# A half tile's rows join the joint expert query, are gathered after it, and 72 instead of 80 hidden blocks are stored

## The chip, the cores and the metric

The kernel runs on one core of one Trainium2 chip. Its metric is the time of one execution in device microseconds. The time before the change is 3701.82 us, the median of three runs (3690.5 to 3702.95).

## The reference

One layer of a hybrid decoder is computed for 1024 prompt tokens and for 64 sample tokens (8 sequences of 8 tokens), with the same weights. What matters here is its expert mixer:

```python
q = (xb @ wq).reshape(PEER_BLOCK, PEER_HEADS, 2, PEER_DKEY // 2)
s = jnp.einsum('phcd,hcnd->phcn', q, keys).astype(jnp.float32)
sv, si = lax.top_k(s, PEER_TOPK)
cand = sv[:, :, 0, :, None] + sv[:, :, 1, None, :]
cv, ci = lax.top_k(cand.reshape(PEER_BLOCK, PEER_HEADS, PEER_TOPK * PEER_TOPK), PEER_TOPK)
...
gsm = jax.nn.softmax(cv, axis=-1)
hval = jnp.einsum('pd,phkd->phk', xb, u_tab[e])
act = (jax.nn.gelu(hval.astype(jnp.float32), approximate=False) * gsm).astype(xb.dtype)
return jnp.einsum('phk,phkd->pd', act, v_tab[e])
```

For each token and each of 8 heads, 16 of 16384 experts are chosen by two lists of 128 keys. Each chosen expert has a row of 1024 numbers in `peer_u` and one in `peer_v`. Ahead of the mixer stand a norm, one input projection, a retention and a recurrence (RWKV) over the tokens, an output projection and a second norm. Behind it stand a gated per-layer embedding and the last norm.

## The kernel before, in words

The 1088 tokens are nine tiles: tiles 0 to 7 of 128 prompt tokens, and tile 8, a half tile of the 64 sample tokens. The kernel treats the tiles in three sets.

- `E0 = [0, 1, 8]`, the early tiles: each has a query of its own (`early_query`, line 1203) and then its experts' rows are **gathered**, all while the recurrence of later tiles runs (generator `early`, line 1251).
- `G1 = [2, 3]`: they take part in the joint query and are gathered late.
- `G2 = [4, 5, 6, 7]`: they take part in the joint query, and their mixer is **dense**: all 16384 experts, in 128 blocks of 128, are multiplied with these 512 tokens, and a table of gates that is zero for experts not chosen weighs them.

A *gather* (`gather`, line 1143) goes over the columns of the index table `eid`. For each, POOL issues one indirect DMA (line 1154) that fetches 128 rows of 1024 numbers, one for each partition. A whole tile has 128 columns in `peer_u` and 128 in `peer_v`. Tile 8 has 64 of each, since its 64 tokens lie twice on the partitions. DVE multiplies a `peer_u` row with the token and sums it (line 1168), and adds a weighted `peer_v` row to the sum `gacc` (line 1182). `gacc` is one buffer in PSUM, so gathers of tiles follow each other. In all there are 1152 gathers.

The stages, in order of time:

1. Projections of all tiles, then the **recurrence** (`group_b`), one tile after another in the order 1, 8, 2, 3, 4, 5, 6, 7. A tile's step finishes its state at line 932. Gathers of tiles 0 and 1 run beside it. Once tile 8's normed rows are there (`self.rowed`), `early` steps tile 8's query between tile 1's gathers (lines 1267 to 1275): 16 products of the half tile with a 1024 x 128 piece of the query weights (line 1232), a product with the keys (line 1235), five DVE instructions a piece that pick the 16 best of 128 (`pick`, lines 1046 to 1050), and the selection (`topk`).
2. The **joint query** (`c_query`, line 1017): for each of 16 pieces of the query weights, which are split into a high and a low part (POOL's `wql`, line 308), one product with the rows of `G1` (256 columns) and one with those of `G2` (512), a product with the keys each, and `pick` for each of the six tiles.
3. The **gates stage** (loop at line 1584). For each tile of `G2`: its selection, and its gates as one-hot products (`oh` on DVE, line 1297; scaling on ACT, line 1299; `pwt` on PE, line 1302; a copy on ACT, line 1303). `NPRE` hidden blocks are spread over it (`hidden`, line 1311): a block's 512 KB of `peer_u` are loaded on SP's queue, split by ACT and POOL (`ul`, line 308), multiplied on PE in 24 matmuls (`ph`) and stored in DRAM (`gd`, line 1591). At `TK1` = step 1 and step 4 the selection and the gather of tiles 2 and 3 are entered.
4. The **fused dense stage** (`dense_fused`): the other 128 - `NPRE` hidden blocks are made and used at once, four to a group, with 24 matmuls `py` each (lines 1353 to 1356).
5. The **stored dense stage** (`dense_stored`): the `NPRE` stored blocks are read back and used, five to a group. A group has 8 slices of `peer_v`; each is split (`vl` on POOL) and its product is added to `yT` on DVE (line 1360).
6. The **last stage** (`ple`): the per-layer embedding and the last norm, tile by tile in the order `E0 + G2 + G1`. The last tile, 3, adds its gathered sum straight from `gacc` (line 1446).

The program is written as Python generators, and a scheduler puts every engine's instructions in a fixed order from them. So what stands next to what on an engine is fixed ahead of the run, and an engine that comes to a gather's sum waits for it.

Of the kernel before, what the change touches and what calls it, by code (L numbers as in the profile page):

```python
# [9 lines left out]
F32 = mybir.dt.float32  # L10
# [3 lines left out]
U32 = mybir.dt.uint32  # L14
AF = mybir.ActivationFunctionType
# [154 lines left out]
PE_ = 0  # L170
PG = 0
PWS = 4
NPRE = 80
NF = 4
TK1 = {2: 1, 3: 4}
GEB = 2
GHB = 2
WQ = 32
# [1 line left out]
WB = 2  # L180
AB = 8
CRING = 4
E0 = [0, 1, 8]
G1 = [2, 3]
DW = 4
LW = 3
CN = 4
# [9 lines left out]
G2 = [4, 5, 6, 7]  # L197
# [3 lines left out]
QB = 4  # L201
SB = 3
EB = 150
SIZE = {t: (64 if t == 8 else 128) for t in range(9)}


def spans(tiles):

    e = [sum(SIZE[t] for t in tiles[:i]) for i in range(len(tiles) + 1)]
    return dict(zip(tiles, e)), e[-1]  # L210
# [8 lines left out]
class K:  # L219
# [797 lines left out]
    def c_query(self, wp, da, parts):  # L1017

        nc, I = self.nc, self.I
        for hc in range(16):  # L1020
            kT = wp.tile([128, 128], F32, name="keysT")
            nc.sync.dma_start(kT, I['keysT'][:, hc])
            raw = da.tile([128, 8, 128], F32, name="wqr", tag="uraw", bufs=UB)
            nc.sync.dma_start(raw, I['wq'][hc])
            wh = da.tile([128, 8, 128], F32R, name="wqh", tag="uh", bufs=DW)
            wl = da.tile([128, 8, 128], F32R, name="wql", tag="ul", bufs=LW)
            self.split(wh, wl, raw, "g")
            for tiles, x in parts:
                off, n = spans(tiles)
                s = wp.tile([128, len(tiles), 128], F32, name=f"ss{tiles[0]}", bufs=SB)  # L1030
                p = self.ps("pq", "b")
                self.mm3(p[:, :n], lambda k: wh[:, k, :], lambda k: wl[:, k, :], lambda k: x[0][:, k], lambda k: x[1][:, k], 8)
                qT = wp.tile([128, n], F32, name=f"qT{tiles[0]}", bufs=1)
                nc.scalar.activation(qT, p[:, :n], AF.Copy)
                p = self.ps("psc", "a")
                for i, t in enumerate(tiles):
                    nc.tensor.matmul(p[:SIZE[t], i * 128:i * 128 + 128], qT[:, off[t]:off[t] + SIZE[t]], kT, start=True, stop=True)
                nc.scalar.activation(s, p[:, :len(tiles) * 128].rearrange("p (t k) -> p t k", k=128), AF.Copy)
                for i, t in enumerate(tiles):
                    self.pick(self.found[t], hc, s[:, i], 128)  # L1040
            yield

    def pick(self, found, hc, s, n):
# [8 lines left out]
    def topk(self, tp, t, s=None, tags={}, ce=None):  # L1052
        nc = self.nc
        n = SIZE[t]
        if s is None:
            sv, si = self.found[t]
        else:
            sv = tp.tile([128, 16, 16], F32, name="sv")
            si = tp.tile([128, 16, 16], U32, name="si")
# [36 lines left out]
        cf = tp.tile([128, 128], F32, name="cf", tag="cf" if ce else "sf")  # L1096
# [9 lines left out]
        if t in G2:  # L1106
            gsm = self.gsm[t] = tp.tile([128, 128], F32, name="gsm", bufs=2)
            self.e12[t] = tp.tile([128, 2, 128], F32, name="e12", bufs=2)
        elif t == 8:
            gsm = tp.tile([128, 128], F32, name="gsm8", tag="cf")  # L1110
        else:
            gsm = self.gsm[t]
        ex = tp.tile([128, 8, 16], F32, name="ex")
# [137 lines left out]
    def early(self, wp):  # L1251

        rows = ("V", "V", "Wq", "Wq", "Wq", "Wq", "W", "xy")
        self.wide = True
        yield from self.early_query(wp, E0[0], "Wq", QB, (("W",), ("xy",)))
        g = self.gather(wp, E0[0], rows, acc=self.acc)
        while E0[1] not in self.rowed:
            next(g, None)
            yield
        self.wide = False  # L1260
        for i, _ in enumerate(self.early_query(wp, E0[1], "Wq", QB, ("Wq", "xT"))):
            if i % 3 == 0:
                next(g, None)
            yield
        yield from g
        g = self.gather(wp, E0[1], rows, acc=self.acc)
        q = None
        for i, _ in enumerate(g):
            yield
            if E0[2] in self.rowed and q is None:  # L1270
                q = self.early_query(wp, E0[2], "Wq", QB, ("Wq", "xT"))
            if q and i % 1 == 0:
                next(q, None)
        for _ in q:
            yield
        self.wide = False
        yield from self.gather(wp, E0[2], rows + ("xT",), acc=self.acc)

    def gates(self, wp, t, extra):
        nc = self.nc  # L1280
# [201 lines left out]
    def build(self):  # L1482
        PS = bass.MemoryType.PSUM
        run = lambda g: [None for _ in g]
        sb = lambda name, es, **kw: self.pool(name, es=es, reuse_waits="tile", **kw)
        with self.es:
            self.setup()
            em, ee, eg, et, ew, ex, ep, e0, e1, e2 = (ExitStack() for _ in range(10))
            acc = self.acc = self.pool("psumg", space=PS, es=eg, reuse_waits="tile")
# [12 lines left out]
            m = mix[0]  # L1502
# [16 lines left out]
            for _ in a:  # L1519
                for _ in range(IE):  # L1520
# [7 lines left out]
            parts = [G1, G2]  # L1528
            self.layout(cq, [(f"ss{g[0]}", [128, len(g), 128], F32, SB) for g in parts] +
                        [(f"qT{g[0]}", [128, spans(g)[1]], F32, 1) for g in parts])  # L1530
            c1 = sb("cx1", ew, side="right")
            x1 = self.rows_of(c1, G1)
            cx = sb("cx2", ex)
# [1 line left out]
            da = sb("dna", eg, bufs=2)  # L1535
            self.layout(da, [("uh", [128, 8, 128], F32R, DW), ("ul", [128, 8, 128], F32R, LW), ("uraw", [128, 8, 128], F32, UB), ("spare", [128, 8, 128], F32, 1)])
            tp = sb("tk", et)
            self.found = {t: (tp.tile([128, 16, 16], F32, name=f"sv{t}"), tp.tile([128, 16, 16], U32, name=f"si{t}")) for t in G1 + G2}
            self.e12 = {}
            n3 = spans(G2[:-1])[1]  # L1540
            query = self.c_query(cq, da, [(G1, x1), (G2, x)])
# [16 lines left out]
            run(ahead)  # L1558
            run(last)
            run(query)  # L1560
            run(early)
            ew.close()
            ee.close()
# [10 lines left out]
            with ExitStack() as e:  # L1574
                self.psums("psumw", e, i=1, w=2)
                self.psh = self.pool("psumh", bufs=3, space=PS, es=e, reuse_waits="tile")
                gw = sb("gw", e, side="right")
                self.stage = (gw, kp)
                self.turn = 0
                self.layout(gw, [("oh", [128, 2, 4, 128], F32, 2), ("it", [128, 128], F32, 2)])  # L1580
                gh = sb("gh", e, bufs=2, side="right")
                gate = iter(())
                nh = 0
                for i, t in enumerate(G2 + [None]):
                    tk = self.topk(tp, t) if t is not None else iter(())
                    while True:
                        a, b = next(tk, "end"), next(gate, "end")
                        if a == "end" and b == "end":
                            break
                    while nh < NPRE * (i + 1) // (len(G2) + 1):  # L1590
                        self.nc.scalar.dma_start(self.gd[nh], self.hidden(da, gh, x, nh))
                        nh += 1
                    gate = self.gates(gw, t, da) if t is not None else gate
                    for t in G1:
                        if i == TK1[t]:
                            run(self.topk(tp, t))
                            run(self.behind(self.gather(gp, t, acc=acc), PG))
            et.close()
            self.first = True
# [31 lines left out]
```

## Time and profile before

| | |
|---|---|
| median of three runs | 3701.82 us |
| profiled execution, its own time | 3682.12 us |
| its span | 3680.3 us |
| PE / DVE / POOL / ACT busy | 89% / 78% / 64% / 33% |
| moved by DMA | 1074.69 MB, 292 GB/s over the span |
| gathers (line 1154) | 1152, from 441.9 to 3635.6 us |
| stored blocks `gd` | 80 of 256 KB |

Times are in microseconds from the start of the span, unless marked as nanoseconds. PE is the matmul engine, and PEld is its weight load, which overlaps it. Matmuls are pipelined, so that a matmul's own duration is longer than the distance to the next. A row of a group gives the line, engine, operation, output and inputs, shapes, the count, then the busy time and the mean duration in nanoseconds, then the engine's idle time ahead of these instructions and what ended it. The granted clock is that of PE, 1.00 being full speed. The DMA share is the mean busy share of the core's 16 DMA engines.

### The profile page before, as it was taken

To read this page: it belongs to the slowest core of one execution; us is meant where nothing else is said; L and a number is where in the kernel's file an instruction comes from. 1 tells how busy PE (TensorE), PEld (TensorE's weight loads), DVE (VectorE), ACT (ScalarE), POOL (GpSimd) and SP (SyncE) were. 2 spreads that over 40 slices of the span, in tenths; PEclk is the share of its full clock that TensorE was granted. 3 is DMA by queue.
4 is the path that set the end of the run, shared out by engine and by line. 5 is a ranking of instruction groups with operands and counts; after the bars stand their busy time and mean duration, and the time that the engine had idled before them with its cause. 6 is when DMAs were issued, how large, how long until landed. Compare 5 with 4: busy or idle time off the path is not lost. (4 is left out here: it accounts for less than half of the span.)

```text
span 3680.3 us, 52362 instructions
## 1 busy us (share of the span) xinstructions
PE 3268.2 (89%) x17749; PEld 2715.5 (74%) x17749; DVE 2857.6 (78%) x5655; ACT 1218.4 (33%) x2259; POOL 2345.1 (64%) x2068
## 2 busy tenths in 40 slices
PE   8798996887968888876989999999999998899988
PEld 7697995654846667655877887887888877667766
DVE  4544689897797886688997999776777787778887
ACT  4233221111211211112333887773333333333322
POOL 5352677554355654436468777768888878887752
PEclk9798996666968885877999999999999999999999
DMA  7257599889858887878678988999999999999974
GB/s 263 86 192 244 200 350 316 277 300 309 280 187 308 311 298 238 300 252 295 206 261 310 324 311 287 345 350 355 342 346 339 332 364 353 369 361 365 340 246 167
DMA packets 423558, 1074.69 MB, mean 292 GB/s; under 512 B 46267, under 2 KB 143289, under 8 KB 418618
## 3 DMA queue, kind: packets, MB, share of 16 engines
q0 software_dynamic: 165888, 604.05, 45.9%
q1 hardware_dynamic: 202670, 377.02, 30.9%
q10 hardware_dynamic: 54732, 90.26, 6.6%
q8 instruction: 141, 2.31, 0.3%
q14 instruction: 127, 1.04, 0.1%
HBM read 980.93 MB, written 90.18 MB: 291 GB/s over the span
## 5 line engine op out<-in xcount | busy, mean ns | idle before, releaser
L1154 POOL DMA_INDIRECT grow<-in_pv,eid x576 | 569.5, 989 | 534.4 <-DVE gacc L1182 299.0
L1154 POOL DMA_INDIRECT grow<-in_pu,eid x576 | 564.2, 979 | 343.1 <-DVE grow L1168 203.2
L1168 DVE SCALAR_TENSOR_TENSOR grow<-grow,gacc 128x1024 f32<-128x1024 f32 x576 | 690.2, 1212 | 116.7 <-DMA grow<-in_pu,eid 114.9
L1182 DVE SCALAR_TENSOR_TENSOR gacc<-grow,ac,gacc 128x1024 f32<-128x1024 f32 x571 | 731.1, 1280 | 33.2 <-DMA grow<-in_pv,eid 28.2
L1353 PE MATMUL py<-ah,vh 128*128 128x512 f32 x1024 | 406.8, 398 | 32.2 <-ACT vh L304 32.2
L333 PE MATMUL ph<-cx,uh 128*128 128x512 f32 x1024 | 406.8, 397 | 7.2 <-DVE al L306 4.6
L334 PE MATMUL ph<-cx,uh 128*128 128x512 f32 x1024 | 405.0, 396 | 0.0
L1354 PE MATMUL py<-al,vh 128*128 128x512 f32 x1024 | 404.7, 395 | 0.0
L308 POOL TENSOR_TENSOR vl<-vraw,vh 128x640 fp32r<-128x640 f32 (+1 forms) x224 | 325.9, 1461 | 39.9 <-ACT vh L304 30.2
L308 POOL TENSOR_TENSOR ul<-uraw,uh 128x1024 fp32r<-128x1024 f32 x128 | 308.1, 2407 | 49.1 <-ACT uh L304 21.0
L1356 PE MATMUL py<-ah,vl 128*128 128x512 f32 x1024 | 272.3, 397 | 13.9 <-POOL vl L308 13.8
L336 PE MATMUL ph<-cx,ul 128*128 128x512 f32 x1024 | 263.4, 395 | 0.0
L1353 PEld LDWEIGHTS py<-ah,vh 128*128 128x128 f32 x1024 | 196.0, 191 | 82.0 <-ACT vh L304 40.3
L304 ACT ACTIVATE vh<-vraw 128x640 fp32r<-128x640 f32 (+1 forms) x224 | 154.8, 692 | 274.3 <-DMA vraw<-in_pvd 95.9
L1356 PEld LDWEIGHTS py<-ah,vl 128*128 128x128 f32 x1024 | 192.3, 189 | 63.3 <-POOL vl L308 21.7
L333 PEld LDWEIGHTS ph<-cx,uh 128*128 128x128 f32 x1024 | 194.8, 190 | 47.0 <-DVE al L306 5.0
L1360 DVE TENSOR_TENSOR yT<-yT,py 128x512 f32<-128x512 f32 x216 | 147.5, 684 | 102.1 <-PE py L1356 101.0
L1354 PEld LDWEIGHTS py<-al,vh 128*128 128x128 f32 x1024 | 195.8, 191 | 41.1
L334 PEld LDWEIGHTS ph<-cx,uh 128*128 128x128 f32 x1024 | 194.5, 190 | 38.5
L336 PEld LDWEIGHTS ph<-cx,ul 128*128 128x128 f32 x1024 | 191.3, 189 | 38.2
L304 ACT ACTIVATE uh<-uraw 128x1024 fp32r<-128x1024 f32 x128 | 135.0, 1056 | 162.0 <-DMA uraw<-in_puT 109.3
L1297 DVE TENSOR_TENSOR oh<-csta,pit 128x1024 f32<-128x1024 f32 x128 | 153.6, 1210 | 27.5 <-ACT oh L1299 17.9
(402 smaller groups left out, 7247.9 us busy)
## 6 DMA issues: line engine op xcount, KB each, us to landing
uraw<-in_puT SPq DMA_DIRECT2D x128, 512.0 KB, 4.2
vraw<-in_pvd SPq DMA_DIRECT2D x128, 320.0 KB, 7.2
cw<-in_w_out SPq DMA_DIRECT2D x128, 256.0 KB, 5.9
wd<-wst ACTq DMA_DIRECT2D x28, 1024.0 KB, 12.3
wt<-wd SPq DMA_DIRECT2D x64, 448.0 KB, 6.8
wraw<-in_w_ret SPq DMA_DIRECT2D x48, 512.0 KB, 4.2
ewq<-in_wq SPq DMA_DIRECT2D x48, 512.0 KB, 5.0
vraw<-in_pvd SPq DMA_DIRECT2D x96, 256.0 KB, 5.4
```

Source lines behind the costliest of these rows:

```text
L304: nc.scalar.activation(hi, src, AF.Copy)
L308: nc.gpsimd.tensor_tensor(lo, src, hi.bitcast(F32), op=OP.subtract)
L333: mm(out, lh(k), rh(k), start=first and k == 0, stop=False)
L334: mm(out, *((ll(k), rh(k)) if right else (lh(k), rl(k))), start=False, stop=False)
L336: mm(out, *((lh(k), rl(k)) if right else (ll(k), rh(k))), start=False, stop=last and k == nk - 1)
L1154: nc.gpsimd.indirect_dma_start(out=g, out_offset=None, in_=src, in_offset=bass.IndirectOffsetOnAxis(ap=self.eid[t][:, j:j + 1], axis=0))
L1168: nc.vector.scalar_tensor_tensor(g[:, c], g[:, c], 1.0, x[:, c], op0=OP.mult, op1=OP.mult, accum_out=hv[:, i, j:j + 1])
L1182: nc.vector.scalar_tensor_tensor(y[:, c], g[:, c], ac[:, j:j + 1], y[:, c], op0=OP.mult, op1=OP.add)
L1297: nc.vector.tensor_tensor(oh, io, p[:, 0:2, s + b:s + b + 4, None].to_broadcast([128, 2, 4, 128]), op=OP.is_equal)
L1353: nc.tensor.matmul(p, vh[:, b, :], ah, start=b == 0, stop=False)
L1354: nc.tensor.matmul(p, vh[:, b, :], al, start=False, stop=False)
L1356: nc.tensor.matmul(p, vl[:, b, :], ah, start=False, stop=b == nb - 1)
```

## The change

Tile 8 leaves the early set and becomes the first of the late set `G1`. Its rows are the first 64 of 320 columns in the joint query's first part. Its scores are copied by an ACT instruction of their own, over 64 partitions, and `pick` works on 64 partitions for it. Its selection is entered right behind the joint query, ahead of what is left of `early`, which is the rest of tile 1's gather. Its gather is entered in the gates stage at step 0, behind the first 14 hidden blocks. Tiles 2 and 3 keep their steps 1 and 4. `NPRE` goes from 80 to 72. So the fused stage has 56 blocks in 14 groups, and the stored stage has 72 in 15 groups, of which the last has two blocks. In the last stage tile 8 now stands behind tiles 4 to 7.

```diff
-NPRE = 80
+NPRE = 72
-TK1 = {2: 1, 3: 4}
+TK1 = {8: 0, 2: 1, 3: 4}
...
-E0 = [0, 1, 8]
-G1 = [2, 3]
+E0 = [0, 1]
+G1 = [8, 2, 3]
...
-                nc.scalar.activation(s, p[:, :len(tiles) * 128].rearrange("p (t k) -> p t k", k=128), AF.Copy)
+                m = len([t for t in tiles if t == 8])
+                for t in tiles[:m]:
+                    nc.scalar.activation(s[:64, 0], p[:64, :128], AF.Copy)
+                nc.scalar.activation(s[:, m:], p[:, m * 128:len(tiles) * 128].rearrange("p (t k) -> p t k", k=128), AF.Copy)
                 for i, t in enumerate(tiles):
-                    self.pick(self.found[t], hc, s[:, i], 128)
+                    self.pick(self.found[t], hc, s[:, i], SIZE[t])
...
-            gsm = tp.tile([128, 128], F32, name="gsm8", tag="cf")
+            gsm = tp.tile([128, 128], F32, name="gsm8", tag="gsm", bufs=2)
...
         g = self.gather(wp, E0[1], rows, acc=self.acc)
-        q = None
-        for i, _ in enumerate(g):
-            yield
-            if E0[2] in self.rowed and q is None:
-                q = self.early_query(wp, E0[2], "Wq", QB, ("Wq", "xT"))
-            if q and i % 1 == 0:
-                next(q, None)
-        for _ in q:
-            yield
         self.wide = False
-        yield from self.gather(wp, E0[2], rows + ("xT",), acc=self.acc)
+        yield from g
...
             run(query)
+            run(self.topk(tp, 8))
             run(early)
...
                         if i == TK1[t]:
-                            run(self.topk(tp, t))
+                            if t != 8:
+                                run(self.topk(tp, t))
                             run(self.behind(self.gather(gp, t, acc=acc), PG))
```

Tile 8's tables of scores found (`sv`, `si`) get a pool of their own, `cf8`, and the rows `cx` of `G1` are 320 wide. Line numbers after the change are 3 higher than before from `pick` on, and 6 lower from `gates` on.

More of the change, by code (lines that the diff above doesn't have):

```diff
@@ L1530, in build @@
                         [(f"qT{g[0]}", [128, spans(g)[1]], F32, 1) for g in parts])
+            cf = sb("cf8", ew, side="right")
             c1 = sb("cx1", ew, side="right")
@@ L1537, in build @@
             tp = sb("tk", et)
-            self.found = {t: (tp.tile([128, 16, 16], F32, name=f"sv{t}"), tp.tile([128, 16, 16], U32, name=f"si{t}")) for t in G1 + G2}
+            self.found = {}
+            for t in G1 + G2:
+                fp = cf if t == 8 else tp
+                self.found[t] = (fp.tile([128, 16, 16], F32, name=f"sv{t}"), fp.tile([128, 16, 16], U32, name=f"si{t}"))
             self.e12 = {}
```

## The prediction

> **What bounds the kernel now.** I read the page first, then the busy time by stretches, then the gathers of each stretch, then the last microseconds. The page gives the span and the share of each engine:
>
> ```profile
> span 3680.3 us, 52362 instructions
> PE 3268.2 (89%) x17749; PEld 2715.5 (74%) x17749; DVE 2857.6 (78%) x5655; ACT 1218.4 (33%) x2259; POOL 2345.1 (64%) x2068
> ```
>
> No engine is full over the whole span, so the change has to be priced stage by stage. These are the stretches: start:end, length, then busy time and count of PE, PEld, DVE, ACT and POOL, the granted clock, the DMA share and GB/s.
>
> ```profile
> 1183.00:1283.00 100.00, 83.55 (x518) 65.70 (x517) 84.69 (x162) 18.48 (x37) 59.55 (x59) 0.86 0.88 309
> 1283.00:1383.00 100.00, 87.48 (x514) 68.41 (x514) 82.21 (x158) 18.51 (x37) 56.11 (x56) 0.83 0.85 295
> 1383.00:1508.00 125.00, 113.96 (x644) 99.59 (x644) 77.25 (x122) 21.65 (x51) 49.00 (x49) 0.67 0.77 264
> 1508.00:1656.00 148.00, 112.72 (x584) 82.96 (x584) 112.52 (x248) 20.20 (x43) 64.14 (x63) 0.75 0.78 264
> 1656.00:1708.00 52.00, 30.51 (x116) 20.60 (x116) 44.71 (x119) 8.62 (x16) 24.37 (x29) 0.70 0.88 317
> 1708.00:1886.00 178.00, 162.00 (x970) 143.67 (x971) 173.67 (x758) 54.96 (x91) 105.83 (x80) 0.95 0.70 226
> 1886.00:2514.00 628.00, 599.98 (x3078) 508.04 (x3077) 521.14 (x1069) 427.97 (x862) 477.83 (x378) 0.98 0.89 322
> 2514.00:2985.00 471.00, 471.00 (x2075) 389.04 (x2074) 361.45 (x491) 146.92 (x219) 403.37 (x328) 1.00 0.96 341
> 2985.00:3519.00 534.00, 487.88 (x2043) 388.31 (x2041) 422.49 (x680) 194.92 (x320) 419.02 (x349) 0.97 0.99 354
> 3519.00:3650.00 131.00, 121.29 (x551) 95.77 (x551) 116.49 (x143) 34.55 (x67) 62.34 (x69) 0.95 0.72 240
> ```
>
> The first four rows are one step each of the recurrence, cut where a tile's state is finished (`S<-S,pe`, line 932: tiles 4, 5, 6, 7). Two steps take 100 us; the two in which tile 8's own query, picks and selection run take 125 and 148. Then follow a tail of 52, the joint query (1708, DVE full: 173.67 of 178), the gates stage (1886), the fused dense stage (2514, PE full), the stored dense stage (2985, DMA at 0.99) and the last stage, the per-layer embedding (3519). The gathers issued by POOL in some of them (busy, count):
>
> ```profile
> 1183.00:1283.00 100.00, 41.90 (x41) 0.86 0.88 309
> 1383.00:1508.00 125.00, 38.46 (x40) 0.67 0.77 264
> 1508.00:1656.00 148.00, 47.51 (x47) 0.75 0.78 264
> 1656.00:1708.00 52.00, 15.35 (x15) 0.70 0.88 317
> 1886.00:2514.00 628.00, 187.26 (x196) 0.98 0.89 322
> 2514.00:2985.00 471.00, 190.80 (x200) 1.00 0.96 341
> 2985.00:3519.00 534.00, 181.78 (x191) 0.97 0.99 354
> 3519.00:3650.00 131.00, 46.55 (x41) 0.95 0.72 240
> ```
>
> The end, on DVE:
>
> ```profile
> 3647.27 1.28 DVE L1182 SCALAR_TENSOR_TENSOR gacc<-grow,ac,gacc 128x1024 f32<-128x1024 f32 x1
> 3650.39 1.21 DVE L1446 TENSOR_TENSOR ph<-ph,gacc 128x1024 f32<-128x1024 f32 x1
> ```
>
> The last gathered row is added at 3647.27, and only then does tile 3's residual sum (line 1446) start, 30 us ahead of the span's end. So the gather chain and the dense work end almost together, and both must be followed.
>
> **The change, part by part.** First, the recurrence loses tile 8's query. Its cost there, PE then DVE:
>
> ```profile
> L1232 PE MATMUL epq<-exT,ewq 128*128 128x64 f32 x256 | 40.1, 321 | 5.4 <-ACT Pi L743 4.7 <-ACT sg L728 0.7
> L1046 DVE MAX8 sv<-es 64x8 f32<-64x128 f32 x16 | 3.6, 269 | 0.0
> L1047 DVE FIND_INDEX8 si<-sv,es 64x8 uint32<-64x128 f32 x16 | 4.3, 275 | 0.0
> L1048 DVE MATCH_REPLACE8 es<-sv,es 64x128 f32<-64x128 f32 x16 | 4.2, 266 | 0.0
> L1049 DVE MAX8 sv<-es 64x8 f32<-64x128 f32 x16 | 3.7, 270 | 0.0
> L1050 DVE FIND_INDEX8 si<-sv,es 64x8 uint32<-64x128 f32 x16 | 4.3, 277 | 0.0
> ```
>
> Its 32 loads on SP's queue, its copies on ACT and its stores there go with it; the joint query loads the same weights anyway, so none comes back. If the last two steps return to 100 us, that is 25 + 48 = 73; the tail also loses the selection, and I take 15 of its 44.71 us of DVE: -88. The low bound is the PE time alone, -40. The high bound goes by gather slots: 102 gathers were issued from 1383 to 1708 in 325 us; in the new POOL order 20 fewer stand ahead of the first joint-query split (451, not 471), and 82 at 100/41 = 2.4 us are 200 us: -125. I stay with the steps, since they are the same work with and without the query. The granted clock is 0.67 and 0.75 in the query's steps and 0.86 and 0.83 in the quiet ones, so the query's extra matmuls did not keep it up. The Trainium skill ("TensorE: Matmul & The Clock Gate", HAM oscillation) says the reverse should be feared: idle gaps of some 3.4 us throttle the clock, and taking matmuls out makes gaps. By the row the term is -88; by the rule some 30 less is saved (worked out from rows in the third rival).
>
> Second, the joint query takes tile 8 in. Its picks come back in a stretch where DVE is full: 20 us by the five rows (they are the same instructions on 64 partitions). Two more row accumulations lie in it (44 gathers, not 42, by the POOL order), 2.6 us. Out of it goes what was left of tile 8's selection there:
>
> ```profile
> L1104 DVE TENSOR_REDUCE ef<-eq 64x16 f32<-64x800 f32 x5 | 4.9, 970 | 1.3 <-POOL eq L1102 1.3
> ```
>
> That is 4.9 us. Sum +17; bounds 0 (hidden in a shorter queue on DVE) and +35 (PE's 16 us of idle time filled by the 64 wider columns as well). So the first hidden block starts 71 us earlier, but with fewer gathers done. On POOL, where `ul` is the split of a hidden block, `eid_65` and `eid_66` are the indices of tiles 1 and 8, before:
>
> ```order
> L308 TENSOR_TENSOR wql<-wqr,wqh 128x1024
> L1154 DMA grow<-in_pv,eid_65 128x1024 x2
> L308 TENSOR_TENSOR wql<-wqr,wqh 128x1024
> L1154 DMA grow<-in_pu,eid_66 128x1024 x3
> L308 TENSOR_TENSOR ul<-uraw,uh 128x1024
> L1154 DMA grow<-in_pu,eid_66 128x1024 x5
> ```
>
> and now, where tile 8's first fetch stands, behind 14 `ul`, its own selection and the start of tile 4's:
>
> ```order
> L308 TENSOR_TENSOR ul<-uraw,uh 128x1024
> L1105 TENSOR_TENSOR eq<-eid,cf 64x800
> L308 TENSOR_TENSOR ul<-uraw,uh 128x1024
> L1074 TENSOR_TENSOR sf<-sf,csta 128x256
> L1082 TENSOR_TENSOR eid<-sf 128x8x16
> L1082 TENSOR_TENSOR eid<-sf 128x8x8
> L1082 TENSOR_TENSOR eid<-sf 128x8x5
> L1082 TENSOR_TENSOR eid<-sf 128x8x4
> L1082 TENSOR_TENSOR eid<-sf 128x8x3
> L1085 TENSOR_TENSOR eid<-sf 128x8x6
> L1089 TENSOR_TENSOR eid<-sf 128x8x8
> L1157 DMA grow<-in_pu,eid_66 128x1024 x5
> ```
>
> At the first `ul` 515 gathers had been issued; now 495, and between tile 1's last gather and tile 8's first stand five `ul` and no gather, while tile 8's selection runs on DVE and POOL.
>
> Third, the gates stage. Its PE rows show a run of 16 one-hot records and where the next starts, and two hidden blocks' last matmuls; its ACT rows are the work of a group of four tokens' gates:
>
> ```profile
> 2352.53 1.95 PE L1302 MATMUL pwt<-oh 128*128 128x128 f32 x16
> 2354.23 0.48 PE L333 MATMUL ph<-cx,uh 128*128 128x512 f32 x1
> ...
> 2356.59 1.98 PE L336 MATMUL ph<-cx,ul 128*128 128x512 f32 x8
> 2362.03 1.99 PE L336 MATMUL ph<-cx,ul 128*128 128x512 f32 x8
> ```
>
> ```profile
> L1299 ACT ACTIVATE oh<-oh,it 128x128 f32<-128x128 f32 x512 | 160.6, 392 | 39.1 <-DVE oh L1297 23.9 <-issue 4.0 <-DVE ef L1104 3.9
> L1303 ACT ACTIVATE wst<-pwt 128x512 f32<-128x512 f32 x127 | 133.6, 1102 | 9.0 <-PE pwt L1302 4.6 <-issue 3.5 <-ACT geh L1322 0.8
> ```
>
> A hidden block takes 5.44 us of PE (2362.03 - 2356.59), and eight one-hot records, one group, take 0.85 (half of 1.70). Eight blocks fewer are 44 us. But the PE order runs dry at the end of the gates. Before (the last one-hot products `pwt` among hidden blocks `ph`):
>
> ```order
> L1302 MATMUL pwt<-oh 128x128 x4
> L334 MATMUL ph<-cx_13100,uh 128x512
> L333 MATMUL ph<-cx_13099,uh 128x512
> L334 MATMUL ph<-cx_13100,uh 128x512
> L336 MATMUL ph<-cx_13099,ul 128x512 x2
> L1302 MATMUL pwt<-oh 128x128 x4
> L336 MATMUL ph<-cx_13099,ul 128x512 x6
> ```
>
> and now:
>
> ```order
> L336 MATMUL ph<-cx_12732,ul 128x512 x6
> L1296 MATMUL pwt<-oh 128x128 x4
> L336 MATMUL ph<-cx_12732,ul 128x512
> L1296 MATMUL pwt<-oh 128x128 x84
> L333 MATMUL ph<-cx_12732,uh 128x512
> ```
>
> The last 21 groups of four have no hidden block beside them. Such a group costs ACT 4 x 0.392 + 1.102 = 2.67 us and PE 0.85, so PE waits about 1.8 x 21 = 38; some of the 28 us that PE idles in this stage now lie in the same place, 7 say: -44 + 38 - 7 = -13. Bounds -44 (no wait) and +10.
>
> Fourth, the dense stages. In the fused one the same matmuls of two blocks stand on PE at:
>
> ```profile
> 2632.91 1.81 PE ph L336 x8
> 2643.82 1.81 PE ph L336 x8
> ```
>
> A fused block takes 10.9 us; eight more: +87. A stored block takes 534/80 = 6.68 us, DMA-bound; eight fewer: -53. By the DVE order a stored block now has 178/72 gathers beside it instead of 191/80, 6 more in all; a gather moves 128 x 1024 words, 0.524 MB, 1.48 us at 354 GB/s: +9. Together +43, bounds +25 and +55. There is one group of slices more (29, not 28), whose eight short DVE sums lie beside PE; eight stores and eight loads of a block fewer are in the 53.
>
> Fifth, the last stage. By the DVE order 45 gathers were left after the last `yT`; now 64, and 13 of them come after all other tiles. DVE's end before:
>
> ```order
> L1182 SCALAR_TENSOR_TENSOR gacc<-grow,ac,gacc 128x1024
> L1470 TENSOR_TENSOR psg<-psg,ppp 128x512
> L1479 SCALAR_TENSOR_TENSOR fin<-ph,frs,row_norm_final 128x512 x2
> L1446 TENSOR_TENSOR ph<-ph,gacc 128x1024
> L1471 TENSOR_TENSOR ph<-ph,psg 128x512
> ```
>
> and now:
>
> ```order
> L1465 TENSOR_TENSOR ph<-ph,psg 128x512
> L1185 SCALAR_TENSOR_TENSOR gacc<-grow,ac,gacc 128x1024 x3
> L1473 SCALAR_TENSOR_TENSOR fin<-ph,frs,row_norm_final 128x512 x2
> L1185 SCALAR_TENSOR_TENSOR gacc<-grow,ac,gacc 128x1024 x13
> L1440 TENSOR_TENSOR ph<-ph,gacc 128x1024
> ```
>
> ```profile
> L1182 DVE SCALAR_TENSOR_TENSOR gacc<-grow,ac,gacc 128x1024 f32<-128x1024 f32 x45 | 57.7, 1281 | 0.6 <-DMA grow<-in_pv,eid 0.5
> ```
>
> DVE had 116.49 of 131 us, 59 of it not gathers. Now 59 + 51 x 1.28 = 124, at the same share 139, and 13 x 1.48 = 19 alone: 158, +27 (bounds +15 and +40).
>
> Sum: -88 + 17 - 13 + 43 + 27 = **-14**. The profiled execution took 3682.1 (1.8 outside its span), which gives 3668; it lies 19.7 below the median 3701.8, and from the median the forecast is 3688. With one term at a time at its bound (but for the gather slots, below), -45 to +34.
>
> **The rivals.** *Freed further* (-60, 3642): the recurrence gains the 125 of the gather slots, and the rest of the sum stands: -51; without PE's wait at the gates' end -82. For it: DVE at 82 to 85% in quiet steps has room. Against: the chain of one step has its own length, and the row of 1383 shows DVE at 77 of 125, so DVE alone did not set it.
>
> *The late gathers end the kernel* (+38, 3740; slower): from 1886 to 3650, 628 gathers took 1764 us, 2.81 each. If that pace is the ring's own, 657 are left now: 1846, and a standstill of five hidden blocks at 5.44, 27: 1873, +109, less 71 for the earlier start. It decides as soon as gathers do not go faster in the last stage than 2.81. For it: line 1446 already waits for the last one. Against: in quiet steps they go at 2.4, and DVE's slots set them.
>
> *The clock stays low* (+16, 3718): at 0.67 instead of 0.845 a step's 85.5 us of PE become 108; a step is then longer by 8 (PE its bound) to 22 (all of PE on the chain), two steps by some 30. For it the rows of 1383 to 1708 (0.67 to 0.75), and the clock gate's rule named above. Against: 0.83 to 0.86 in the quiet steps, which have the same gaps.
>
> **How the numbers follow.** Forecast 0.57, freed further 0.16, late gathers 0.17, low clock 0.10. About half a percent, 18.5 us, is what a measurement can tell from no change. Of the forecast's 0.57, 0.24 is faster than that, 0.30 within, 0.03 slower; freed further is faster; late gathers slower; of the low clock 0.06 within, 0.04 slower. Faster 0.40, same 0.36, slower 0.24. The range reaches from the middle of freed further (-65, 3637) to past the late gathers (+45, 3747).
>
> **What would show it.** Two equal steps near 100 us ending the recurrence and a first hidden block near 1815; DVE full in the joint query for about 195 us; 21 one-hot groups at the gates' end at 2.7 us or more with PE idle; the fused stage 87 longer, the stored 44 shorter; some 60 gathers after the last `yT`. I am wrong if the last steps stay over 110, or if the gates stage grows, or if the last stage grows by over 40.

## The result and the profile after

The kernel after the change takes 3653.07 us, the median of four runs (3639.03 to 3657.16), against 3699.44 us for the kernel before on the same chip (3690.5 to 3702.95). The ratio is 0.9864, with a 95% interval from 0.9827 to 0.9900, so 1.4% faster. In a later measurement, with other runs of both kernels, it was 3635.01 against 3680.33, ratio 0.9866 (0.9835 to 0.9897). The forecast was 3688.

The profiled execution of the kernel after took 3657.16 us. From its page, the span and the engines:

```profile
span 3655.2 us, 51715 instructions
PE 3242.7 (89%) x17493; PEld 2685.5 (73%) x17493; DVE 2842.8 (78%) x5663; ACT 1215.9 (33%) x2247; POOL 2343.4 (64%) x2076
```

The shares are those of before, so this view tells nothing of where the time came from. The stretches do. They are cut at the same events as in the prediction: the states of tiles 4, 5, 6 and 7, the first split of the joint query, the first hidden block, the first `py`, the last `ph`, the last `yT`, and tile 3's residual sum (line 1440 now). The columns are length, then busy time and count of PE, PEld, DVE, ACT and POOL, then granted clock, DMA share and GB/s.

```profile
1298.00:1400.00 102.00, 90.73 (x507) 71.38 (x505) 81.24 (x155) 18.61 (x37) 55.81 (x55) 0.78 0.82 287
1400.00:1513.00 113.00, 96.29 (x527) 77.24 (x526) 89.79 (x151) 21.46 (x40) 58.82 (x59) 0.74 0.82 290
1513.00:1580.00 67.00, 60.41 (x395) 50.94 (x396) 53.20 (x71) 11.75 (x20) 34.66 (x33) 0.87 0.81 276
1580.00:1628.00 48.00, 32.73 (x135) 19.01 (x136) 33.62 (x42) 9.47 (x16) 17.06 (x19) 0.86 0.96 366
1628.00:1816.00 188.00, 179.74 (x1006) 155.92 (x1006) 180.07 (x850) 55.94 (x104) 91.80 (x70) 0.97 0.62 201
1816.00:2415.00 599.00, 562.08 (x2887) 475.31 (x2887) 503.39 (x1112) 419.68 (x854) 456.54 (x367) 0.98 0.87 311
2415.00:2971.00 556.00, 556.00 (x2449) 459.24 (x2448) 422.30 (x601) 173.17 (x258) 474.84 (x388) 1.00 0.96 339
2971.00:3464.00 493.00, 448.15 (x1860) 348.87 (x1859) 396.48 (x649) 179.37 (x297) 390.81 (x332) 0.98 0.99 358
3464.00:3624.00 160.00, 123.41 (x570) 96.29 (x568) 143.51 (x168) 37.02 (x70) 81.98 (x90) 0.91 0.78 263
```

Read rows two and three against the 125 and 148 of before. The last step of the recurrence did not fall to the quiet 100: it fell to 67, while the step ahead of it stayed at 113, over the 110 that the prediction had named as a sign of being wrong. That was the first sign that the 88 us had another cause than the one I had priced. The gathers in four of these stretches (POOL busy, count):

```profile
1816.00:2415.00 599.00, 167.53 (x176) 0.98 0.87 311
2415.00:2971.00 556.00, 223.55 (x236) 1.00 0.96 339
2971.00:3464.00 493.00, 172.43 (x182) 0.98 0.99 358
3464.00:3624.00 160.00, 67.60 (x60) 0.91 0.78 263
```

And the end on DVE, where tile 3's sum still comes right behind the last gathered row:

```profile
3620.15 3.94 DVE L1185 SCALAR_TENSOR_TENSOR gacc<-grow,ac,gacc 128x1024 f32<-128x1024 f32 x3 [0.93 <-DMA grow<-in_pv,eid]
3624.12 1.22 DVE L1440 TENSOR_TENSOR ph<-ph,gacc 128x1024 f32<-128x1024 f32 x1
```

Between the profiled executions, term by term (the last column is the second profile of the same kernel after):

| stage, by its marks | before | after | difference | forecast | difference, second profile |
|---|---|---|---|---|---|
| tile 5's state to first split | 325.0 | 227.4 | -97.6 | -88 | -100.4 |
| joint query | 178.2 | 188.4 | +10.2 | +17 | +9.8 |
| gates | 628.1 | 599.0 | -29.1 | -13 | -23.3 |
| fused | 468.9 | 556.2 | +87.3 | +87 | +87.4 |
| stored | 535.5 | 492.1 | -43.4 | -44 | -46.4 |
| last | 131.6 | 160.6 | +29.0 | +27 | +32.3 |
| behind it | 29.9 | 31.1 | +1.2 | 0 | +1.0 |
| sum | | | -42.4 | -14 | -39.6 |

The spans differ by 25 only, since the profiled execution of after was 17 us late already at tile 5's state, up to which both kernels have the same order; in the second profile that was 6 us. The sums from tile 5 on agree with the 46 us between the medians.

### The profile page after: what moved, and what is told of

Read it like the earlier page. It is cut to its first block, busy times and chain, and to the rows that moved or that the text cites. A ratio compares the mean times of both kernels' runs of the same rounds, so it can differ in the third digit from the quotient of the medians.

```text
span 3655.2 us, 51715 instructions
## 1 busy us (share of the span) xinstructions
PE 3242.7 (89%) x17493; PEld 2685.5 (73%) x17493; DVE 2842.8 (78%) x5663; ACT 1215.9 (33%) x2247; POOL 2343.4 (64%) x2076
## 5 line engine op out<-in xcount | busy, mean ns | idle before, releaser
L308 POOL TENSOR_TENSOR vl<-vraw,vh 128x512 fp32r<-128x512 f32 (+2 forms) x232 | 327.5, 1416 | 31.1 <-ACT vh L304 19.9
L304 ACT ACTIVATE vh<-vraw 128x512 fp32r<-128x512 f32 (+2 forms) x232 | 156.1, 675 | 280.0 <-PE py L1348 99.0
L336 PEld LDWEIGHTS ph<-cx,ul 128*128 128x128 f32 x1024 | 191.4, 189 | 43.4 <-POOL ul L308 5.4
L1296 PEld LDWEIGHTS pwt<-oh 128*128 128x128 f32 x1024 | 143.4, 201 | 47.8 <-ACT wst L1297 19.1
```

Of the source, the lines that this page charges most:

```text
L304: nc.scalar.activation(hi, src, AF.Copy)
L308: nc.gpsimd.tensor_tensor(lo, src, hi.bitcast(F32), op=OP.subtract)
L336: mm(out, *((lh(k), rl(k)) if right else (ll(k), rh(k))), start=False, stop=last and k == nk - 1)
```

## The experiments

My theory at this point was that of the prediction: the recurrence lost the PE and DVE work of the half tile's query (*work theory*), and the blocks were a second, separate trade. Each kernel was timed against runs of the kernel before on the same chip; the medians of before were 3670.03 beside the first four kernels, 3672.91 beside the next four and 3680.33 beside the last four.

**The two parts of the change alone.** First, the kernel after with 80 stored blocks, so that only the half tile moves:

```diff
-NPRE = 72
+NPRE = 80
```

> The changed kernel with 80 stored blocks again, so only tile 8's move is left. Theory (the move frees the recurrence, and 72 blocks then give the late gathers time): against the changed kernel the fused stage is 87 us shorter (8 x 10.9), the stored one 53 longer, the gates stage 30 to 44 longer, and the last stage 20 to 30 longer, since by the DVE order 80 gathers, not 64, are left after the last yT: some 25 us slower than the changed kernel, 20 us faster than before (about 3680). Rival (the 72 blocks carry nothing, the move all of it): as fast as the changed kernel, about 3653. Rival (the 72 blocks carry it all): about 3700.

Measured: 3631.96 (3621.47 to 3635.91), ratio 0.9894 (0.9845 to 0.9943). Then the other part, the kernel before with 72 blocks (`NPRE = 80` becomes 72):

> The kernel before with 72 stored blocks, the other part of the change alone. Theory: fused +87, stored -53, gates -44 and some 15 of waits back, last stage -5 (41 gathers left after the last yT, not 45): 0 to +5 us, no change from before (about 3700). Rival (the 72 blocks carry the gain by themselves): 20 us or more faster than before.

Measured: 3670.11, ratio 0.9987 (0.9958 to 1.0016). So the half tile's move carries the gain, and the blocks nothing that can be seen, in either kernel. In the kernel before that could be a sum of small terms. In the kernel after it could not: fused and stored together are 51 us shorter with 80 blocks (469.0 + 528.0 against 556.2 + 492.1), and yet the time did not fall. I come back to that below.

**The query's work.** The kernel before with two of the eight matmuls in each product of the half tile's own query (six left out, so it picks other experts):

```diff
-            for k in range(8):
+            ks = (0, 7) if t == 8 else range(8)
+            for k in ks:
```

> The kernel before with only two of the eight matmuls in each product of tile 8's own query (its scores are then those of a quarter of the rows); loads, picks and selection stay. Theory (PE's and DVE's time for tile 8 both lengthen the last two steps of the recurrence): PE loses 30 of its 40 us, and the stretch from tile 5's step to the joint query's first split goes from 325 us to about 295; whole kernel 20 to 30 us faster. Rival (only DVE's picks and selection count): the stretch stays over 315. Rival (the clock): the granted clock falls below 0.67 in these steps and nothing is saved.

Measured: 3678.01, ratio 1.0005 (0.9966 to 1.0044). And the kernel before with the picks of one of the 16 pieces only, copied to the other 15:

```diff
-            for hc in range(16):
+            for hc in range(1 if t == 8 else 16):
...
+            if t == 8:
+                nc.vector.tensor_copy(sv[:n, 1:16], sv[:n, 0:1].to_broadcast([n, 15, 16]))
+                nc.vector.tensor_copy(si[:n, 1:16], si[:n, 0:1].to_broadcast([n, 15, 16]))
```

> The kernel before with tile 8's picks made for one of 16 score pieces and copied to the others (so all its heads choose alike); its matmuls, loads and the selection stay. Theory: DVE loses some 22 us where it is 76% busy, and the stretch from tile 5's step to the joint query goes from 325 to about 305; whole kernel 10 to 20 us faster. Rival (only PE's matmuls count): the stretch stays over 315. Rival (loads and the chain of one step set it): both this and the kernel with a quarter of the matmuls stay over 315.

Measured: 3666.49, ratio 1.0006 (0.9978 to 1.0034). Neither the PE time nor the DVE time that I had priced is worth anything by itself. The stretch from tile 5's state to the first split, 325 us before, took 319 and 334. The steps of the kernel with a quarter of the matmuls, in stretches:

```profile
1380.00:1482.00 102.00, 87.96 (x472) 77.76 (x470) 64.20 (x105) 19.95 (x46) 39.05 (x39) 0.65 0.77 259
1482.00:1643.00 161.00, 113.67 (x561) 78.89 (x560) 120.39 (x260) 21.72 (x48) 70.93 (x70) 0.76 0.81 274
```

Tile 6's step became quiet, 102 us, but tile 7's took 161 instead of 148: 13 of the 23 us that were saved came back one step later. Taken one part at a time, the work theory does not hold.

**What holds tile 7 back.** A tile's front begins with the product `pz` (line 725). In the timeline of PE in the kernel before, it starts when tile 6's state products `pS` are long done:

```profile
1505.11 0.44 PE L921 MATMUL pS<-U,nbk 128*128 128x128 f32 x2
...
1506.73 0.39 PE L922 MATMUL pS<-vtk,ktk 128*128 128x128 f32 x2
...
1525.10 1.02 PE L725 MATMUL pz<-w2aug,tw 65*128 65x512 f32 x2
```

In the kernel after it starts 29 us ahead of the same products:

```profile
1478.60 1.02 PE L725 MATMUL pz<-w2aug,tw 65*128 65x512 f32 x2
...
1507.65 0.79 PE L921 MATMUL pS<-U,nbk 128*128 128x128 f32 x2
```

So before, the front of tile 7 did not overlap with the back of tile 6, and tile 7's step had to hold both. The program shows a tie that neither matmul time nor picks explain. `pz` takes its PSUM tile from a ring named `a`, which has two banks. So do the transposes `etr` and products `epq` of the half tile's query, and the ring is claimed in the order in which the generators ask. These are the claims on `a` between the last transpose of tile 6's front (`trn`) and tile 7's `pz`, before and after:

```
before: etr etr epq epq epq epq pgt epq tr epq tr epq pin pin epq etr epq etr po epq ewo epq pst epq ewo epq | pz
after:  pgt tr tr pin pin etr etr po ewo pst ewo | pz
```

26 claims, of which 15 are the query's, against 11. An `epq` tile is held through a product, a copy on ACT, the product with the keys and a second copy on ACT. The *ring theory*: tile 7's `pz` waits its turn in two banks behind 15 such claims, however short the work in them is. Four kernels tell it from the work theory and from each other.

The kernel before without the half tile's query (its experts and gates are copied from 64 columns of tile 1's; its gathers stay early) gives the price of the whole:

```diff
-        q = None
-        for i, _ in enumerate(g):
...
-        for _ in q:
-            yield
+        yield from g
+        self.nc.vector.tensor_copy(self.eid[8], self.eid[1][:, :64])
+        self.nc.vector.tensor_copy(self.gsm[8], self.gsm[1][:, :64])
```

> Kernel before without the half tile's own query: its expert numbers and gates are copied from the first 64 columns of tile 1's, its 128 gathers stay early (so the half tile's rows come from other experts; 72 against 80 blocks untouched: 80). Every theory on the recurrence that lays the 98 us on something in that query expects the whole of it here: tile 7's `pz` 25 to 40 us before tile 6's state step, the last two steps 185 to 205 us together instead of 273, and, as nothing else of the kernel before is changed, 85 to 105 us off its time (ratio 0.971 to 0.977). If the recurrence was shortened by the later place of the half tile's gathers instead, nothing moves (ratio 0.997 to 1.003).

Measured: 3630.10, ratio 0.9871 (0.9839 to 0.9902). The last two steps took 184.5 us and tile 5's state to the first split 242.1, as expected; but the time fell by 43 us, not by 85 to 105.

The kernel before with the query whole, on the other ring:

```diff
-            p = self.ps("etr", "a").rearrange("p (a b) -> p a b", a=4)
+            p = self.ps("etr", "b" if t == 8 else "a").rearrange("p (a b) -> p a b", a=4)
...
-            p = self.ps("epq", "a")
+            p = self.ps("epq", "b" if t == 8 else "a")
```

> Kernel before with the half tile's query as it is, all its matmuls and picks, but its PSUM tiles (`etr`, `epq`) taken from the ring `b` of three banks instead of the ring `a` of two, where the tile fronts take theirs in the order of the program. Ring theory (18 turns of the query stand ahead of tile 7's `pz` in the two banks of `a`, each held through two matmul groups and two ScalarE copies): `pz` of tile 7 comes 20 to 35 us before tile 6's state step again, the last two steps take 190 to 225 us instead of 273, the joint query starts 45 to 85 us earlier, and the time falls by 40 to 85 us (ratio 0.977 to 0.989), less what the query's turns cost the solves in `b`, of which 10 to 20 us are allowed for. Work theory (the recurrence is longer by the query's PE and DVE time): nothing moves, since all that work is still there: last two steps 265 to 280, ratio 0.997 to 1.003.

Measured: 3661.37, ratio 0.9969 (0.9943 to 0.9996). Its last two steps, and `pz` on PE:

```profile
1389.00:1520.00 131.00, 118.48 (x781) 96.31 (x779) 103.95 (x262) 27.16 (x67) 54.47 (x52) 0.90 0.79 278
1520.00:1588.00 68.00, 60.21 (x369) 50.60 (x369) 51.92 (x75) 11.97 (x20) 33.49 (x35) 0.79 0.80 265
```

```profile
1466.72 1.02 PE L725 MATMUL pz<-w2aug,tw 65*128 65x512 f32 x2
1508.24 0.80 PE L921 MATMUL pS<-U,nbk 128*128 128x128 f32 x2 [0.68 <-ACT U L916]
```

All of the query's matmuls and picks are still there, and the step that had been 148 is 68: that is the ring theory's sign. The step with the query's work is 131, some 20 more than the 108 and 113 without it: that is what is left of the work theory. The recurrence gained 73 us (252.4 against 325.0). The time gained only 0.3%, less than I had expected.

Then the other way round: the kernel after, with 18 turns added where the query's were, each of two matmuls of constants and two ACT copies that nobody reads; in one kernel on ring `a`, in the other on ring `b`:

```diff
-        yield from g
+        turns = iter(range(18))
+        for _ in g:
+            yield
+            if 8 in self.rowed and next(turns, None) is not None:
+                p = self.ps("epq", "a")
+                nc, one = self.nc, self.c("ident")
+                nc.tensor.matmul(p[:, :64], one, one[:, :64], start=True, stop=True)
+                qT = wp.tile([128, 128], F32, name="eqT", tag="cf")
+                nc.scalar.activation(qT[:, :64], p[:, :64], AF.Copy)
+                nc.tensor.matmul(p[:64, 128:256], qT[:, :64], one, start=True, stop=True)
+                st = wp.tile([128, 2, 128], F32, name="es", tag="sv")
+                nc.scalar.activation(st[:64, 0], p[:64, 128:256], AF.Copy)
```

> Kernel after with 18 empty turns added in the ring `a` at the places where the kernel before took the query's: each is a matmul of 128x64, a copy of 64 columns, a matmul of 64x128 and a copy, of constants, into tiles that nobody reads: 18 x 2 x some 0.2 us of PE, no loads, no picks. Ring theory: tile 7's `pz` goes behind tile 6's state step again, the last two steps rise from 179 to 235 to 275 us, and most of the gain is lost: ratio to the kernel before 0.993 to 1.005. Work theory (PE, DVE, loads): less than 10 us of work is added, so the time stays that of the kernel after, ratio 0.982 to 0.990, last two steps 180 to 190.

> The same 18 empty turns in the kernel after, but in the ring `b`. Ring theory: `pz` of tile 7 stays some 30 us ahead of tile 6's state step, last two steps 180 to 200, ratio to the kernel before 0.982 to 0.992. If what delays the front is the ScalarE copies or the mere number of instructions in the queues, this kernel loses as much as the one with the turns in `a`: last two steps 235 to 275, ratio 0.993 to 1.005.

Measured: on `a` 3680.50, ratio 1.0006 (0.9978 to 1.0034); on `b` 3638.62, ratio 0.9884 (0.9848 to 0.9920). The same instructions, on another ring, make the whole difference between keeping the gain and losing it. With the turns on `a`, the last two steps, and PE where `pz` stands:

```profile
1387.00:1514.00 127.00, 116.04 (x494) 97.23 (x494) 77.38 (x122) 21.30 (x53) 49.70 (x50) 0.53 0.63 211
1514.00:1629.00 115.00, 101.38 (x511) 73.58 (x509) 92.22 (x117) 20.03 (x43) 59.78 (x60) 0.79 0.90 306
```

```profile
1512.21 0.39 PE L922 MATMUL pS<-vtk,ktk 128*128 128x128 f32 x2
1512.52 0.43 PE L1280 MATMUL epq<-csta,eqT 128*64 128x128 f32 x2
...
1524.61 0.43 PE L1277 MATMUL epq<-csta 128*128 128x64 f32 x2 [0.36 <-ACT es L1282]
1525.89 0.43 PE L1280 MATMUL epq<-csta,eqT 128*64 128x128 f32 x2
1526.69 1.12 PE L725 MATMUL pz<-w2aug,tw 65*128 65x512 f32 x2 [0.37 <-ACT es L1282]
```

The last of these rows has the tie in it: `pz` was released by `es`, the copy that frees the bank of the turn ahead of it. With the turns on `b`:

```profile
1397.00:1513.00 116.00, 108.44 (x596) 85.09 (x596) 94.02 (x151) 27.04 (x64) 62.92 (x60) 0.78 0.82 289
1513.00:1574.00 61.00, 53.39 (x369) 43.40 (x368) 46.15 (x63) 11.21 (x19) 29.55 (x30) 0.92 0.82 274
```

The two steps are 242 us with the turns on `a`, 177 with them on `b`, and 180 without.

**The clock beside the ring.** These two kernels differ in the granted clock as well. The stretch from 1440 to 1500, first with the turns on `a`, then on `b`:

```profile
1440.00:1500.00 60.00, 60.00 (x266) 53.24 (x265) 28.32 (x36) 11.96 (x32) 15.93 (x17) 0.50 0.54 175
1440.00:1500.00 60.00, 58.96 (x330) 45.67 (x332) 43.02 (x66) 15.88 (x39) 30.08 (x31) 0.84 0.90 316
```

With the turns on `a`, PE was busy for all of these 60 us at half its clock, and 266 matmuls are recorded against 330: successive `pZG` start 0.217 us apart there, and 0.110 where the kernel with `b` has the full clock. Weighed with the clock granted at each moment, PE's busy time in the two steps is 143 us of full-speed work on `a` and 134 on `b`. But 150 us of it ran at 0.50 on `a`, and 57 on `b`. Half of that difference, 46 us, is what the lower clock cost: the larger part of the 65 us between 242 and 177. More work and more idle time are 9 each. Between the kernel before and the query on ring `b` (168 and 155 us of full-speed work, 117 and 48 us at 0.50) it is some 35 of 74. So the ring decides, but how it makes the steps longer is not settled: by the order alone, or by the low clock that came with that order. No kernel here changed the clock alone.

**Where dense time goes.** Three results asked for one more theory: 51 us of dense time that were worth nothing, and two kernels that gained 83 and 73 us in the recurrence and only 43 and 11 in the time. My *gather theory* was that the 1152 gathers, one behind another, set the end, so that dense time is hidden. Against it stands the *dense theory*, that of the prediction's sum: the lengths of the stages add up. Four kernels test it: the kernel after itself, with 80 blocks, with 48 blocks, and with 72 blocks but 24 of tile 1's 128 experts left out, which are 48 early gathers less:

```diff
+        cut = 104 if t == E0[1] else n
...
-        for j in range(n):
+        for j in range(cut):
             g = fetch(I['pu'], j)
...
-        for j in range(n):
+        for j in range(cut):
             g = fetch(I['pv'], j)
```

> The kernel after itself, beside the next three on one chip: ratio to the kernel before 0.983 to 0.990, as in the first measurement.

> The kernel after with 80 stored blocks instead of 72. Gather theory (the 1152 gathers, one after another, set the end; dense time is hidden as long as gathers are left over behind it): 43 us of dense time saved come back in the last stage, the time within 8 us of the kernel after. Dense theory (the sum of my prediction, fused +87, stored -44): 43 us below the kernel after, less 15 at most in the last stage, that is 28 to 43 us.

> The kernel after with 48 stored blocks instead of 72: by the change's own rates (10.9 us for each block moved into the fused stage, 5.4 us off the stored stage) 24 x 5.5 = 132 us more dense time. Gather theory: the last stage of 161 us shrinks to 30 to 60 us, and the time rises by 0 to 30 us only. Dense theory: the time rises by 100 to 132 us.

> The kernel after with 24 of the 128 experts of tile 1 left out, so 48 of the 1152 gathers, all of them before 1850 us and well ahead of the hidden blocks. Gather theory: every later gather comes that much sooner, the last stage falls from 60 gathers behind the last `yT` to 10 to 25, and the time falls by 70 to 125 us although nothing is changed in the last 1700 us. Dense theory: the hidden blocks and the output loop keep their times, and the kernel gains 0 to 25 us.

| kernel | median, us | ratio to before | fused + stored | last stage | gathers behind the last `yT` |
|---|---|---|---|---|---|
| after, 72 blocks | 3635.01 | 0.9866 (0.9835 to 0.9897) | 1045.4 | 163.9 | 60 |
| after, 80 blocks | 3641.36 | 0.9880 (0.9851 to 0.9909) | 998.1 | 191.0 | 76 |
| after, 48 blocks | 3691.65 | 1.0030 (1.0006 to 1.0053) | 1176.6 | 111.7 | 16 |
| after, 48 gathers less | 3628.69 | 0.9834 (0.9791 to 0.9876) | 1048.9 | 160.4 | 57 |

With 80 blocks, 47 us of dense time came back in full: 27 in the last stage and 21 in the gates stage (625.5 against 604.8), which has eight blocks more to make. With 48 blocks, 131 us more dense time cost 57 us: 52 were taken from the last stage and 38 from the gates stage, and 10 were added behind tile 3's sum. Both speak for gathers at the end, but the second lies between what the two theories expected, 0 to 30 and 100 to 132: the last stage stops shrinking. Its row in the kernel with 48 blocks, last `yT` to tile 3's sum:

```profile
3534.00:3646.00 112.00, 106.59 (x499) 83.92 (x498) 84.05 (x111) 33.03 (x62) 28.87 (x43) 0.98 0.50 164
```

PE is busy for 106.59 of 112 us, so little is left to save in it while PE's work stays the same. The kernel after has 49 us more than that, for its gathers; the kernel before had 20.

With 48 early gathers less the theory failed outright: 6 us instead of 70 to 125, inside the 0 to 25 of the dense theory. POOL's gathers in that kernel ahead of and inside the joint query (busy, count) show why:

```profile
1618.00:1654.00 36.00, 12.77 (x14) 0.91 0.83 288
1654.00:1805.00 151.00, 0.52 (x1) 1.00 0.20 66
```

The early gathers had run out at 1654, and the next one started at 1854.6, when the half tile's experts were known: 201 us without a gather. In the kernel after, the same wait is 28 us (gathers 512 and 513, at 1859 and 1888). My reading is that what ends the kernel after is not the chain of all 1152 gathers, but the 640 that have to wait for the joint query. They run from 1888 to 3617 us, 2.70 us each. The gathers ahead of them just fill the time until then. No further kernel was made for this reading, but the two with empty turns bear it out: with the turns on `a` the 640 start at 1921, on `b` at 1876, both run at 2.72 us each, and where the starts differ by 45 us the times differ by 42.

## Why the prediction was right, and where it was not

The range held the time, and the sign was right. The forecast itself was 35 us too high, and the time lies nearer to the 3642 of *freed further*, 11 us away. That the sum came so near in its largest terms was in part luck, since the largest of them had the wrong reason.

**Recurrence.** The size held (-98 for -88), the reason did not. The step that failed is the one that took the query's PE and DVE time for the cause: "If the last two steps return to 100 us". They did not return to 100; they became 113 and 67 (108 and 68 in the second profile), and the mark that I had set, two equal steps, missed. With the matmuls quartered or the picks cut to one piece nothing was gained; with the whole query on another ring 73 us were, which leaves some 25 of the 98 for the query's own work. The prediction read PE as busy for 113.96 of 125 us and looked for what filled it. PE was busy, but with `pz` of the next tile held behind the query's claims in its order, and for long at half its clock: of 227 busy us in the two steps, 117 were at 0.50, against 64 of 157 in the kernel after. The prediction had the low clock in its rows and did not ask where it came from. The Trainium skill ("Perfetto Trace Analysis", Optimization Strategy) says that the same gap repeating on the engine that should be saturated can mean too little PSUM for the next tile. Here PE had no such gap ahead of `pz` (busy for 40.00 of 40 us from 1425 to 1465 in the kernel before), and it was two banks shared with the filler all the same.

**Joint query.** +10 for +17, inside the bounds; DVE is busy 180.07 of 188.

**Gates.** -29 and -23 for -13. The term that was mis-sized is the price of a one-hot group at the end. The groups of instructions there, 2342 to 2388 us of the kernel after, PE's first and then ACT's:

```profile
L1296 PE MATMUL pwt<-oh 128*128 128x128 f32 x167 | 31.8, 354 | 15.8 <-ACT oh L1293 10.3 <-ACT wst L1297 3.8 <-ACT uh L304 1.5
...
L1293 ACT ACTIVATE oh<-oh,it 128x128 f32<-128x128 f32 x80 | 24.9, 405 | 0.0
L1297 ACT ACTIVATE wst<-pwt 128x512 f32<-128x512 f32 x22 | 22.8, 1068 | 3.0 <-issue 2.1 <-PE pwt L1296 0.8
```

The 21 groups took 2.2 us each, not 2.67. I had multiplied the mean duration of an `oh`, 0.392, by four. But successive ones overlap: 24.9 / 80 is 0.311 us of busy time each, and the row that I had quoted, 160.6 for 512, said 0.314. With busy times the group is 4 x 0.314 + 133.6 / 127 = 2.31. PE's wait is then 21 x (2.31 - 0.85), 31 us, by the forecast's own working and not 38, and the term -20. The stretch itself was 46 us long, 28 more than 21 x 0.85, which makes the term -23, as the second profile has it. The 6 us more of the first were not traced.

**Fused and stored.** +87 and -43, as forecast. But they were added to the others as if they were worth their length, and the kernels with 80 and 48 blocks show that they are not: eight blocks more or fewer leave the time within the intervals.

**Last stage.** +29 for +27, with 60 gathers behind the last `yT`. The right size again came with an incomplete reason: by the reading above, what is left at the end is fixed by when the 640 late gathers could start and by their pace, so that a dense stage that is shortened lengthens this one, as with 80 blocks.

**The rivals.** *The late gathers end the kernel* was right in its first half, by the reading above. It failed in its premise, that the pace is fixed at 2.81 us: with the gather counts above a gather took 3.40 us in the gates stage (599/176), 2.36 in the fused one (556/236) and 2.7 in the last. *The clock stays low* did not come: the last two steps had 0.74 and 0.87, before 0.67 and 0.75, with fewer matmuls in them. The rule of the Trainium skill ("TensorE: Matmul & The Clock Gate", HAM oscillation) is about idle gaps; PE's idle time in the two steps fell too, from 46 to 23 us, so this trace does not decide on it. The lowest clock of all these steps, 0.53, was in the kernel with empty turns on ring `a`, where PE was busy for 116.04 of 127 us. *Freed further* asked for 125 us in the recurrence, and 98 to 100 came. What else lay below the forecast came from the gates (16 and 10 us in the two profiles) and the joint query (7).

**Not settled.** Why the query on ring `b` gives 11 us while no query gives 43 is only argued: both end their last stage at 172 to 177 us, bound by gathers, and the one with the query issues 78 gathers between tile 5's state and the first split where the other issues 87. Its gathers of tiles 2 and 3 start at 2309 us, those of the other at 2245. Whether the order or the low clock carries the loss on ring `a` is open too. No version that leaves nothing out and is faster than the kernel after was found: the query on ring `b`, the one that the ring theory pointed to, is slower than it, and 80 blocks are the same.

## What to carry to other kernels

When work is moved out of a stage, ask what it claims there in order, not only what it occupies: a ring of two banks shared by a critical chain and a filler makes the chain wait for the filler's turns, even empty ones, while the engine looks busy. To test for it, move the filler to another ring, or put empty turns in, and read the granted clock beside the busy time: here the two changed together. And before adding up stages, find which chain ends the kernel and what it is anchored to: 47 us of dense time were worth nothing here, which fits 640 gathers that start behind the joint query and set the end, and 48 gathers ahead of that point were worth about 6 us.

## What was not expected of the hardware

A gather of 128 rows of 1024 numbers went fastest beside the heaviest matmul work: 2.36 us each in the fused stage, where PE was busy all the time and the DMA engines at 0.96, against 3.40 in the gates stage at 0.87 and 3.84 in the joint query (188/49) at 0.62. So a busy PE and busy DMA engines did not slow it. DVE, which every gather needs, was busy 422.30 of 556 us in the first of these stretches and 180.07 of 188 in the last; that its free slots set the pace fits these rows, but was not tried by itself.

A PE that was busy without a break ran on at half its clock: 0.50 over 60.00 busy of 60 us with empty turns on ring `a`, and over 40.00 of 40 from 1425 to 1465 in the kernel before, where the kernel with the query on ring `b` had 1.00 over 37.76 of 40.
